# S5's outer products and the weights' sums on GpSimd, two generators for S5's constants, and a tail with GLU and projection A as separate stages

## The chip, the cores and the metric

The kernel runs on one core of one Trainium2 chip. The metric is the device time of one execution in microseconds (us); lower is better. One core has a matrix engine (TensorE, in the rows PE, its weight loads PEld), a vector engine (VectorE, DVE), a scalar engine (ScalarE, ACT), GpSimd (POOL) and a queue that only issues transfers (SyncE, SP). Each works through its own instructions in the order in which the program issued them; semaphores join them.

## The reference, cut to what matters

One layer of a hybrid encoder, for one prompt of 2048 frames and for eight streams of 16 frames, 1024 channels wide.

```python
h = rmsnorm(x, ln_g)
u_a, z_a, u_b, z_b, g_a, g_b = split(h @ w_in)        # 512 512 1024 1024 1024 1024 columns
y_a, s5_new = s5_mixer(u_a, s5_h0, ...)               # 32 groups of 16 channels, 64 complex states
y_a = gelu(y_a)
y_a = y_a * sigmoid(y_a @ w_glu + b_glu)              # GLU
p_a = (y_a * silu(z_a)) @ w_pa                        # projection A
xc, conv_new = causal_conv(u_b, conv_buf, conv_w, conv_b)
y_b, lru_new = rglru(xc, lru_h0, wa, ba, wx, bx, lam)
p_b = (y_b * silu(z_b)) @ w_pb                        # projection B
m = sigmoid(g_a) * p_a + sigmoid(g_b) * p_b
out = rmsnorm(x + m @ w_out, final_gain)
```

## The kernel before

Every product is made of three float16 matmuls, high by high, high by low and low by high (lines 161 to 163). The frames lie in five tiles, four of 512 columns (n = 0 to 3) and one of 128 for the streams (n = 4). The stages follow each other on PE:

1. **Norm and u_a** (lines 533 to 599). For each tile n and each of four column blocks m, `proj` makes a block of u_a. In the blocks m = 2 and 3 the next tile is transposed by `trans_tile`, two of its eight slabs k in the middle of the block's product (the argument `between`) and two behind it, all through the three PSUM buffers "a". Meanwhile `params` makes S5's parameters, on GpSimd for the most part.
2. **Direct gate blocks** (lines 1308 to 1355). Four columns of gate B, while `t_forms` builds sums of the frames for what follows. `lru_states` (line 648) brings the old states into place by transposes into one PSUM buffer; its copy into `dT` stands between the first transpose and the next.
3. **Branch B** (`run_pair`, lines 1361 to 1396). Sixteen pairs of column blocks, in turn one of branch B ("b") and one of gates ("g"). A pair has 15 slots: seven products of a Winograd scheme over the frames' first half, one slot for the streams, seven products for the second half; a product is 12 matmuls of 512 columns. The weights of the next pair are loaded at slot 5 (`load_pair`) and made into eight forms by `w_forms` (line 778) from slot 8 on: four sums of 128x512 by `tt` on DVE, each then split by ACT (`high`) and DVE (`low`).
4. **S5 beside projection B** (lines 1639 to 1685). For each tile and eight blocks m a product with w_pb; between them come the sixteen `s5_run` tasks, one for two groups each. The loop behind it, `while tasks or low or due`, goes on until every task is over, and so does `tail_start`, which waits for all `s5_run` tasks and then loads w_out and makes `glu_prep(0)`.
5. **Tail** (lines 1704 to 1833). `glu_prep(n)` splits S5's output into high and low; `ga_tile(n)` makes four GLU blocks and then eight blocks of projection A; `out_tile(n)` makes the output product, 24 matmuls for each half row block. The order of tiles is 0, 1, 4, 2, 3, and `BESIDE` says what runs beside which output tile.

Work beside the products is dealt out by a planner. `pump(budget)` (line 683) runs what is due, then lets the generators in `tasks`, and then those in `low`, issue their next piece until the budget of the slot is spent; a yielded number or `Step` costs that much of it, and `Later(k)` lets k turns pass at no cost. In `low` stand `w_spill` (line 1140, 44 blocks of later weights, loaded, split and stored to DRAM) and two generators `s5_prep` (line 1203), which make the constants of the sixteen `s5_run` tasks: parameters are loaded; `outer` (line 1234) makes "wb" and later "wc", each by four products of 128x256 and one sum of 128x512; "wb" is transposed on PE; "wc" is multiplied on PE (line 1282); the result is split, stored to `kpD` by GpSimd (line 1296), and read back by SP as `dd` (line 1301). An `s5_run` task starts when its constants are in the set `prepared`. The second generator waits until branch B is over. `place` is the slot in a b pair (1 to 15) or 15 more in a g pair (16 to 30); `NO_SPILL` and `NO_PREP` are places at which these generators rest.

Of the kernel before, what the change touches and what calls it, by code (L numbers as in the profile page):

```python
# [17 lines left out]
P = 128  # L18
# [29 lines left out]
def build(tc, I, O):  # L48
# [30 lines left out]
    with ExitStack() as es:  # L79
# [121 lines left out]

        def proj(W, n, tag="mm", between=None):
            p = ps(tag)[:, :TILES[n][1]]
            for k in range(KB):
                passes(p, W(k), hT(n, k), k == 0, k == KB - 1)
                if k == 3 and between:
                    between()
            return p
# [9 lines left out]
        with ExitStack() as p1x:  # L218
# [66 lines left out]
            def trans_tile(n, ks=range(KB)):  # L285
                t0, w = TILES[n]
                for k in ks:
                    pt = ps("ab"[k % 2])[:, :w]
                    for i in range(w // P):
                        transp(pt[:, P * i:P * i + P], xts[n, i][:, P * k:P * k + P])  # L290
                    evac_h(n, k, pt)
# [255 lines left out]
            for n in range(4):  # L547
# [8 lines left out]
                for m in range(4):  # L556
                    early = n < 3 and m >= 2
                    p = proj(lambda k: wua[m][:, k], n,
                             between=(lambda: trans_tile(n + 1, range(4 * m - 8, 4 * m - 6))) if early else None)
                    if 0 < n < 3 and m == 1:  # L560
# [16 lines left out]
                    if n < 3:  # L577
                        if m == 0:
                            st = stats()
                            for i in range(4):  # L580
                                norm_sums(n + 1, i, st)
                        if n == 0 and m == 1:
                            norm_root(1, st)
                        if m == 1:
                            for i in range(4):
                                norm_scale(n + 1, i, st)
                            if n == 0:
                                split_ua(3)
                        if m >= 2:
                            trans_tile(n + 1, range(4 * m - 6, 4 * m - 4))  # L590
                    if n == 0 and m == 3:
# [56 lines left out]
        def lru_states():  # L648
            pp = ps("b")
            transp(pp[0:64, 256:272], dn)  # L650
            V.tensor_copy(out=dT, in_=pp[0:64, 256:272])
            transp(pp[:, 0:64], rows2)
            for i in range(2):
                transp(pp[:, 64 + 96 * i:160 + 96 * i], rows3[i])
            ts(lrs[:, 0:64], pp[:, 0:64], LS)
            V.tensor_copy(out=lrs[:, 64:256], in_=pp[:, 64:256])
# [121 lines left out]
        def w_forms(raw, W):  # L778
# [17 lines left out]
            high("A11", A11)  # L796
            tt(t, A21, A22, ADD)
            yield 0.7
            low("A11", A11)
            high("S1", t)  # L800
            yield 0.7
            low("S1", t)
            tt(t, t, A11, SUB)
            high("A12", A12)
            yield 1.3
            low("A12", A12)
            high("S2", t)
            yield 0.7
            low("S2", t)
            tt(t, A12, t, SUB)  # L810
            yield 1.3
            high("A21", A21)
            high("S4", t)
            yield 0.2
            low("A21", A21)
            tt(A21, A11, A21, SUB)
            low("S4", t)
            yield 2.0
            high("S3", A21)
# [316 lines left out]

        NO_SPILL = range(15, 22)
        NO_PREP = range(13, 22)

# [55 lines left out]
        def scratch(nm):  # L1195

            if nm == "t":
                return temp[:, 0:512].rearrange("p (j g h t) -> p j g h t", j=2, g=2, h=16)
            if nm == "w":
                return temp[:, 512:1024].rearrange("p (a r c) -> p a r c", a=2, r=2)  # L1200
            return temp[:, 1024:1280].rearrange("p (r c) -> p r c", r=2)

        def s5_prep(second):
# [9 lines left out]
            dd = None  # L1213
            while second and branch_b:
                yield Later(1)
            while todo:
# [17 lines left out]
                def outer(nm, pr_, pi_, m1, m2):  # L1234
                    w_ = gt([P, 2, 2, 16, 8], name=nm)
                    t = gt([P, 2, 2, 16, 8], name="t") if branch_b else scratch("t")
                    for dst, po, mo in ((w_, pr_, m1), (t, pi_, m2)):
                        for j in range(2):
                            if nm == "wb":
                                pe = pw_(po, 8 - 8 * j, 16 - 8 * j)[:, :, ::-1]  # L1240
                            else:
                                pe = pw_(po, 8 * j + 1, 8 * j + 9)
                            tt(dst[:, j], pe[:, :, None, :].to_broadcast([P, 2, 16, 8]),
                               mat(mo)[:, :, :, None].to_broadcast([P, 2, 16, 8]), MUL)
                    tt(w_, w_, t, ADD)
                    return w_.rearrange("p j g h t -> p j g (h t)")
# [3 lines left out]
                wb = outer("wb", O_PR, O_PI, O_B, O_BS)  # L1250
                yield Step(2.2)
                yield Later(1)
                p = ps("a", (P, 4, P))
# [13 lines left out]
                wc = outer("wc", O_PR, O_PI, O_C, O_CS)  # L1267
                yield Step(2.8)
                yield Later(1)
                wcs = gt([P, 2, 2, 2, P], F16, name="wcs")  # L1270
# [341 lines left out]
        def glu_prep(n):  # L1612
# [4 lines left out]
            for m in range(4):  # L1617
# [9 lines left out]
                yield  # L1627

        def tail_start():

            while len(tasks) > 1 or done["spill"] < 44:
                yield Later(1)
            for i in range(4):
                wo.append(page_load(page_b("t1", (2, 2, D), "wo"), woD[i]))
                yield Later(1)
            for _ in glu_prep(0):
                yield Step(1.4)
# [48 lines left out]
        load_w(wpa, wpaD[1])  # L1686
        so2 = out_states2()

# [14 lines left out]

        def ga_tile(n):
            w = TILES[n][1]
            zq = [tload(zaD, m, n, "qz") for m in range(2)]
            yA[n] = page_a("h", (4, 2, w), "yA") if n < NT - 1 else gt([P, 4, 2, w], F16, "yA")
            for m in range(4):
# [12 lines left out]
                parts(yA[n][:, m], z, 1.0)  # L1721
                yield
            flush()
            gq = [(tload(gaD, m, n, "ga"), tload(mbD, m, n, "mb")) for m in range(2)]
# [74 lines left out]

        def chain(*gens):  # L1800
            for g in gens:
                yield from g

        flush()
        ahead = glu_prep(1)
        for i, _ in enumerate(ga_tile(0)):
# [5 lines left out]
            if i > 7:  # L1812
                next(ahead, None)


        BESIDE = {0: ([1], 2, [4, 2]), 1: ([4, 2], 3, [3]), 4: ([], 0, []), 2: ([3], 2, []), 3: ([], 0, [])}
        for n in TAIL:
            flush()
            gas, steps, preps = BESIDE[n]
            nxt = chain(*[ga_tile(x) for x in gas])  # L1820
            ahead = chain(*[glu_prep(x) for x in preps])
            for i, _ in enumerate(out_tile(n)):
                pump(0)
                for _ in range(steps):
                    next(nxt, None)
                    pump(0)
                if i > 3 or len(preps) > 1:
                    next(ahead, None)
            for _ in nxt:
                pump(0)  # L1830
            for _ in ahead:
                pump(0)
# [33 lines left out]
```

## Time and profile before

| | us |
|---|---|
| median of three timed runs | 1571.83 (1568.13 to 1572.23) |
| profiled execution, device time | 1577.57 |
| its span, first to last instruction | 1575.8 |
| PE busy in the span | 1462.2 (93%) |
| DVE busy | 1039.9 (66%) |
| ACT busy | 816.1 (52%) |
| POOL busy | 275.3 (17%) |

The busy time of PE counts an instruction from its start to its modelled end; matmuls overlap, so a long instruction of 0.38 us may be followed by the next after 0.22 us. [...] What a stage loses is its idle PE time and, of the busy time, the share by which the clock was below 1.00.

### The profile page before, as it was taken

How to read it: one execution, taken by the hardware profiler on the slowest of the kernel's cores; microseconds unless marked ns; L12 is line 12 of the kernel's file. 1: busy time of each engine (PE TensorE's matmuls, PEld its weight loads, DVE VectorE, ACT ScalarE, POOL GpSimd, SP SyncE). 2: the span in 40 equal slices, each digit the busy share in tenths (PEclk: the TensorE clock that was granted, in tenths of full speed). 3: DMA queues.
4: the chain of work that ended last, by engine and by line, in shares of the span. 5: the costliest groups of instructions: out<-in, count | busy, mean ns of one | idle time of the engine just before them, and what ended most of it. 6: DMA issues, size and time to landing. Idle time of an engine off the chain costs nothing.

```text
span 1575.8 us, 22665 instructions
## 1 busy us (share of the span) xinstructions
PE 1462.2 (93%) x8168; PEld 735.3 (47%) x8168; DVE 1039.9 (66%) x2137; ACT 816.1 (52%) x1524; POOL 275.3 (17%) x557
## 2 busy tenths in 40 slices
PE   5989999999999899999999999999983789989997
PEld 3544445444444454444444444555463334444443
DVE  5445785778786677869788784656544776657543
ACT  6542434766767385876867581433234443533322
POOL 0591010120202011110201112334333000000000
PEclk9889999999999999999999999999995889999999
DMA  8216212332422233331413369985856805333431
GB/s 204 85 59 235 81 62 79 98 126 65 139 66 106 86 104 121 102 123 61 156 61 103 110 227 320 331 282 161 308 175 227 310 1 187 99 123 120 174 108 54
DMA packets 168489, 222.20 MB, mean 141 GB/s; under 512 B 39258, under 2 KB 117738, under 8 KB 166328
## 3 DMA queue, kind: packets, MB, share of 16 engines
q1 hardware_dynamic: 144440, 150.96, 29.8%
q0 software_dynamic: 23936, 69.79, 11.9%
q8 instruction: 64, 1.05, 0.3%
q14 instruction: 49, 0.40, 0.1%
HBM read 133.85 MB, written 86.84 MB: 140 GB/s over the span
## 4 chain that ended last, share of the span: by engine, by line
PE 71%; DVE 9%; ACT 6%; DMA 6%; issue 5%; SPq 1%; POOL 1%; DVEq 0%; ACTq 0%; POOLq 0%
PE ps_mm L161 18%; PE ps_mm L162 18%; PE ps_mm L163 18%; PE ps_mm L1775 3%; PE ps_mm L1773 3%; PE ps_mm L1774 3%; DMA wraw<-w_in 1%; PE ps_a L172 1%; ACT L74 1%; DVE yh L53 1%; PE ps_a L1282 1%; DVE xc L65 1%; PE ps_a L162 1%; PE ps_a L161 1%; PE ps_a L163 1%
## 5 line engine op out<-in xcount | busy, mean ns | idle before, releaser
L161 PE MATMUL ps_mm<-T,wf 128*128 128x512 f16 x512 | 194.8, 380 | 11.6 <-ACT ub L74 8.1
L163 PE MATMUL ps_mm<-T,wf 128*128 128x512 f16 x512 | 194.6, 380 | 1.0 <-DVE wf L65 1.0
L162 PE MATMUL ps_mm<-T,wf 128*128 128x512 f16 x512 | 194.7, 380 | 0.0
L162 PEld LDWEIGHTS <-wf 128*128 128x128 f16 x1232 | 120.8, 98 | 124.7 <-issue 15.7
L161 PEld LDWEIGHTS <-wf 128*128 128x128 f16 x1232 | 120.7, 98 | 117.2 <-issue 5.0
L163 PEld LDWEIGHTS <-wf 128*128 128x128 f16 x1232 | 120.8, 98 | 116.6 <-DVE wf L65 2.6
L161 PE MATMUL ps_mm<-h,wf 128*128 128x512 f16 x448 | 170.6, 381 | 2.0 <-ACT wf L74 2.0
L163 PE MATMUL ps_mm<-h,wf 128*128 128x512 f16 x448 | 170.4, 380 | 0.7 <-DVE wf L65 0.7
L162 PE MATMUL ps_mm<-h,wf 128*128 128x512 f16 x448 | 170.5, 381 | 0.0
L1775 PE MATMUL ps_mm<-wo,M 128*128 128x512 f16 (+2 forms) x264 | 99.2, 377 | 5.3 <-DVE M L65 5.3
L1773 PE MATMUL ps_mm<-wo,M 128*128 128x512 f16 (+2 forms) x264 | 99.1, 377 | 0.0
L1774 PE MATMUL ps_mm<-wo,M 128*128 128x512 f16 (+2 forms) x264 | 99.0, 376 | 0.0
L161 PE MATMUL ps_mm<-Y,wpb 128*128 128x512 f16 x256 | 97.8, 382 | 0.0
L163 PE MATMUL ps_mm<-Y,wpb 128*128 128x512 f16 x256 | 97.7, 382 | 0.0
L162 PE MATMUL ps_mm<-Y,wpb 128*128 128x512 f16 x256 | 97.6, 381 | 0.0
L74 ACT ACT_TABLE_LOAD x62 | 79.5, 1283 | 6.1 <-PE ps_mm L163 4.3
L65 DVE SCALAR_TENSOR_TENSOR gb<-gb,ps_mm 128x512 f32<-128x512 f32 (+1 forms) x40 | 24.2, 605 | 86.5 <-PE ps_mm L163 63.9
L74 ACT ACTIVATE gs<-ps_mm 128x512 f32<-128x512 f32 (+1 forms) x92 | 48.5, 537 | 55.6 <-PE ps_mm L163 54.4
L65 DVE SCALAR_TENSOR_TENSOR xc<-ub,PC,xc 128x512 f32<-128x512 f32 x96 | 71.8, 749 | 2.6 <-ACT xc L74 0.3
L65 DVE SCALAR_TENSOR_TENSOR xo<-ps_mm,xo 128x512 f32<-128x512 f32 (+2 forms) x35 | 23.9, 681 | 73.8 <-PE ps_mm L1775 73.7
L65 DVE SCALAR_TENSOR_TENSOR wf<-wraw,wf 128x512 f16<-128x512 f32 (+1 forms) x82 | 55.7, 696 | 17.4 <-ACT wf L74 17.2
L162 PE MATMUL ps_mm<-yA,wt 128*128 128x512 f16 (+1 forms) x160 | 55.7, 356 | 11.0 <-DVE yA L65 7.1
(326 smaller groups left out, 3301.5 us busy)
## 6 DMA issues: line engine op xcount, KB each, us to landing
wraw<-w_in SPq DMA_DIRECT2D x38, 512.0 KB, 4.2
sp<-sD SPq DMA_DIRECT2D x16, 768.0 KB, 5.1
xt<-x_prompt SPq DMA_DIRECT2D x16, 512.0 KB, 4.2
gbD<-gs POOLq DMA_DIRECT2D x32, 256.0 KB, 2.3
ybD<-y POOLq DMA_DIRECT2D x32, 256.0 KB, 3.0
gaD<-gs POOLq DMA_DIRECT2D x32, 256.0 KB, 2.5
Y<-ybD SPq DMA_DIRECT2D x8, 1024.0 KB, 11.1
gb<-gbD SPq DMA_DIRECT2D x32, 256.0 KB, 6.9
```

Of the source, the lines that this page charges most:

```text
L53: V.tensor_tensor(out=out, in0=a, in1=b, op=op)
L65: V.scalar_tensor_tensor(out=out, in0=a, scalar=s, in1=b, op0=op0, op1=op1)
L74: S.activation(out=out, in_=a, func=f, **kw)
L161: PE.matmul(p, lhsT=a[:, 0], rhs=b[:, 0], start=first, stop=False, skip_group_check=more)
L162: PE.matmul(p, lhsT=a[:, 0], rhs=b[:, 1], start=False, stop=False, skip_group_check=more)
L163: PE.matmul(p, lhsT=a[:, 1], rhs=b[:, 0], start=False, stop=last, skip_group_check=more)
L172: PE.matmul(out, lhsT=in_, rhs=ident[0:k, 0:k], start=True, stop=True, is_transpose=True)
L1282: PE.matmul(o[:, 16 + P * j:16 + P * j + w], lhsT=lb, rhs=wc[:, j, g].rearrange("p (h t) -> p t h", t=8)[:, 0:w // 16], start=True, stop=True)
L1773: PE.matmul(p, lhsT=lh[0], rhs=w_[:, 0, c], start=(k == 0), stop=False)
L1774: PE.matmul(p, lhsT=lh[0], rhs=w_[:, 1, c], start=False, stop=False)
L1775: PE.matmul(p, lhsT=lh[1], rhs=w_[:, 0, c], start=False, stop=(k == KB - 1))
```

## The change

- `proj` loses `between`; `trans_tile` makes four slabs in a row behind the blocks m = 2 and 3, and takes its PSUM buffers from "a" and "mm" in turn.
- In `lru_states` the copy to `dT` moves behind all transposes.
- The four sums of `w_forms` go to GpSimd (`gtt` for `tt`), and their costs in the planner fall by 2.4 for a pair in all.
- All products and sums of `outer` go to GpSimd; the planner is charged 3.6 instead of 7.8 for a task's constants, and three turns pass before PE uses a product. Their scratch "t" is always a tile of its own.
- The second `s5_prep` starts as soon as one set of constants is prepared, in branch B.
- `NO_SPILL` grows from places 15 to 21 to 13 to 21, `NO_PREP` from 13 to 21 to 11 to 21.
- `tail_start` prepares tiles 0 and 1. `ga_tile` is cut into `glu_tile` and `pa_tile`; the tail starts with GLU of tiles 0 and 1, then projection A of tile 0 with the preparation of tiles 4 and 2 beside it, then two blocks of projection A of tile 1, then the output tiles. `out_states2` moves from ahead of the tail to behind its third GLU block.

```diff
-        def proj(W, n, tag="mm", between=None):
+        def proj(W, n, tag="mm"):
             p = ps(tag)[:, :TILES[n][1]]
-            for k in range(KB):
-                passes(p, W(k), hT(n, k), k == 0, k == KB - 1)
-                if k == 3 and between:
-                    between()
+            gemm(p, W, lambda k: hT(n, k), KB)
...
-                    pt = ps("ab"[k % 2])[:, :w]
+                    pt = ps(("a", "mm")[k % 2])[:, :w]
...
-                            trans_tile(n + 1, range(4 * m - 6, 4 * m - 4))
+                            trans_tile(n + 1, range(4 * m - 8, 4 * m - 4))
...
             transp(pp[0:64, 256:272], dn)
-            V.tensor_copy(out=dT, in_=pp[0:64, 256:272])
             transp(pp[:, 0:64], rows2)
             for i in range(2):
                 transp(pp[:, 64 + 96 * i:160 + 96 * i], rows3[i])
+            V.tensor_copy(out=dT, in_=pp[0:64, 256:272])
...
-            tt(t, A21, A22, ADD)
-            yield 0.7
+            gtt(t, A21, A22, ADD)
+            yield 0.1
...
-            tt(t, t, A11, SUB)
+            gtt(t, t, A11, SUB)
...
-            tt(t, A12, t, SUB)
+            gtt(t, A12, t, SUB)
...
-            tt(A21, A11, A21, SUB)
+            gtt(A21, A11, A21, SUB)
...
-        NO_SPILL = range(15, 22)
-        NO_PREP = range(13, 22)
+        NO_SPILL = range(13, 22)
+        NO_PREP = range(11, 22)
...
-            while second and branch_b:
+            while second and not prepared:
                 yield Later(1)
...
-                            tt(dst[:, j], pe[:, :, None, :].to_broadcast([P, 2, 16, 8]),
+                            gtt(dst[:, j], pe[:, :, None, :].to_broadcast([P, 2, 16, 8]),
                                mat(mo)[:, :, :, None].to_broadcast([P, 2, 16, 8]), MUL)
-                    tt(w_, w_, t, ADD)
+                    gtt(w_, w_, t, ADD)
...
                 wb = outer("wb", O_PR, O_PI, O_B, O_BS)
-                yield Step(2.2)
-                yield Later(1)
+                yield Later(3)
...
                 wc = outer("wc", O_PR, O_PI, O_C, O_CS)
-                yield Step(2.8)
-                yield Later(1)
+                yield Step(0.8)
+                yield Later(2)
...
-            for _ in glu_prep(0):
+            for _ in chain(glu_prep(0), glu_prep(1)):
                 yield Step(1.4)
...
+        pa = {n: pa_tile(n) for n in TAIL}
+        for i, _ in enumerate(chain(glu_tile(0), glu_tile(1))):
             pump(0)
             if i < 2:
                 xload(i)
+            if i == 2:
+                so2 = out_states2()
+        ahead = chain(glu_prep(4), glu_prep(2))
+        for i, _ in enumerate(pa[0]):
+            pump(0)
+            next(ahead, None)
             if i == 1:
                 out_states3(so2)
+        for _ in range(2):
+            next(pa[1])
+            pump(0)
...
-        BESIDE = {0: ([1], 2, [4, 2]), 1: ([4, 2], 3, [3]), 4: ([], 0, []), 2: ([3], 2, []), 3: ([], 0, [])}
+        BESIDE = {0: (pa[1], glu_tile(4), glu_tile(2)), 1: (pa[4], pa[2]), 4: (glu_tile(3),), 2: (pa[3],), 3: ()}
```

## Rows read from the trace of the kernel before

**Rows 1.** Windows: length, busy us (instructions) of each engine, granted clock, DMA share.
```profile
36.00:147.00 111.00, 98.06 (x526) 52.48 (x526) 52.84 (x127) 48.76 (x95) 62.73 (x176) 0.89 0.29 103
147.00:300.00 153.00, 147.14 (x780) 70.64 (x781) 111.24 (x192) 68.88 (x124) 14.60 (x27) 0.97 0.29 93
300.00:958.00 658.00, 644.30 (x3609) 317.20 (x3608) 507.68 (x935) 459.34 (x803) 104.92 (x194) 1.00 0.34 114
958.00:1166.00 208.00, 203.80 (x1365) 112.58 (x1363) 113.42 (x326) 66.46 (x174) 72.27 (x122) 0.99 0.78 267
1166.00:1225.00 59.00, 24.66 (x229) 21.36 (x230) 24.55 (x86) 21.54 (x54) 18.77 (x32) 0.65 0.66 220
1225.00:1290.00 65.00, 54.62 (x219) 22.36 (x218) 49.58 (x76) 28.34 (x38) 1.05 (x2) 0.84 0.48 173
1290.00:1420.00 130.00, 121.44 (x642) 58.41 (x641) 79.95 (x180) 53.14 (x100) 0.00 (x0) 0.95 0.37 129
```

**Rows 2.** Who PE waited for, 1166 to 1225: total us, times, longest.
```profile
PE ps_a L1486 <- ACT hst L74: 18.8, 3, 10.0
PE ps_mm L161 <- ACT yh L74: 8.9, 1, 8.9
```

**Rows 3.** Line 1282, eight matmuls a task's constants: 250 to 960, then 960 to 1225.
```profile
L1282 PE MATMUL ps_a<-wc,par x80: 382/386/413, 270.6 to 947.6; 128*32 128x128 f32 x40, 128*32 128x112 f32 x40
...
L1282 PE MATMUL ps_a<-wc,par x48: 382/386/413, 1054.3 to 1169.5; 128*32 128x128 f32 x24, 128*32 128x112 f32 x24
```

**Rows 4.** Who PE waited for, 36 to 147.
```profile
PE ps_a L172 <- DVE xt L69: 13.2, 4, 8.3
```

**Rows 5.** Who PE waited for, 147 to 300.
```profile
PE ps_a L172 <- DVE dTe L651: 3.8, 1, 3.8
```

**Rows 6.** Who PE (first row) and ACT (other rows) waited for, 300 to 958.
```profile
PE ps_mm L161 <- ACT ub L74: 8.1, 5, 4.7
...
ACT wf L74 <- DVE wt L53: 19.0, 13, 6.2
...
ACT wq L74 <- DMA wr<-w_pb: 8.2, 1, 8.2
```

**Rows 7.** DVE groups by shape: count, busy us, mean ns, idle before.
```profile
L53 DVE TENSOR_TENSOR wt<-wt,wraw 128x512 f32<-128x512 f32 x16 | 11.1, 692 | 0.6
...
L53 DVE TENSOR_TENSOR wc<-par 128x256 f32<-128x256 f32 x32 | 12.0, 415 | 0.0
```

**Rows 8.** POOL groups by shape, the same columns.
```profile
L56 POOL TENSOR_TENSOR e<-pw 128x256 f32<-128x256 f32 x4 | 2.6, 657 | 0.2
...
L56 POOL TENSOR_TENSOR bst<-e 128x512 f32<-128x512 f32 x1 | 1.3, 1267 | 0.1
```

**Rows 9.** SP's own waits over the span, then SP's issues in order of time.
```profile
SPq L1301 <- DMA kpD<-kf: 214.7, 16, 34.1
...
522.97 2.73 SPq L1301 DMA_DIRECT2D dd<-kpD  x4
525.80 1.16 SPq L144 DMA_DIRECT2D wraw<-w_in  x2
```

**Rows 10.** DVE, then POOL, in order of time: start, us.
```profile
91.51 0.68 DVE L65 SCALAR_TENSOR_TENSOR sp_t<-sp_t 128x8 f32<-128x8 f32 x1
...
91.45 0.72 POOL L56 TENSOR_TENSOR pw<-e 128x256 f32<-128x256 f32 x1
```

**Rows 11.** DVE groups by shape, 1225 to 1290.
```profile
L53 DVE TENSOR_TENSOR yh<-ya,yh 128x256 f16<-128x256 f32 x15 | 17.1, 1314 | 0.0
L65 DVE SCALAR_TENSOR_TENSOR gl<-gl,ya 128x256 f32<-128x256 f32 x12 | 6.7, 602 | 7.2 <-ACT gl L74 7.0
```

**Rows 12.** Who PE waited for, 1225 to 1420.
```profile
PE ps_mm L1775 <- DVE M L65: 5.3, 3, 2.1
```

**Rows 13.** PE in order of time: start and modelled length of two matmuls.
```profile
1151.34 0.38 PE L161 MATMUL ps_mm<-Y,wpb 128*128 128x512 f16 x1
1151.56 0.38 PE L162 MATMUL ps_mm<-Y,wpb 128*128 128x512 f16 x1
```

More of the change, by code (lines that the diff above doesn't have):

```diff
@@ L556, in build @@
                 for m in range(4):
-                    early = n < 3 and m >= 2
-                    p = proj(lambda k: wua[m][:, k], n,
-                             between=(lambda: trans_tile(n + 1, range(4 * m - 8, 4 * m - 6))) if early else None)
+                    p = proj(lambda k: wua[m][:, k], n)
                     if 0 < n < 3 and m == 1:
@@ L802, in w_forms @@
             low("S1", t)
-            tt(t, t, A11, SUB)
+            gtt(t, t, A11, SUB)
             high("A12", A12)
-            yield 1.3
+            yield 0.7
             low("A12", A12)
@@ L809, in w_forms @@
             low("S2", t)
-            tt(t, A12, t, SUB)
-            yield 1.3
+            gtt(t, A12, t, SUB)
+            yield 0.7
             high("A21", A21)
@@ L815, in w_forms @@
             low("A21", A21)
-            tt(A21, A11, A21, SUB)
+            gtt(A21, A11, A21, SUB)
             low("S4", t)
-            yield 2.0
+            yield 1.4
             high("S3", A21)
@@ L1195, in scratch @@
         def scratch(nm):
-            if nm == "t":
-                return temp[:, 0:512].rearrange("p (j g h t) -> p j g h t", j=2, g=2, h=16)
             if nm == "w":
@@ L1235, in outer @@
                     w_ = gt([P, 2, 2, 16, 8], name=nm)
-                    t = gt([P, 2, 2, 16, 8], name="t") if branch_b else scratch("t")
+                    t = gt([P, 2, 2, 16, 8], name="t")
                     for dst, po, mo in ((w_, pr_, m1), (t, pi_, m2)):
@@ L1627, in glu_prep, with chain @@
                 yield
+        def chain(*gens):
+            for g in gens:
+                yield from g
         def tail_start():
@@ L1686, in build @@
         load_w(wpa, wpaD[1])
-        so2 = out_states2()
         def parts(d, t, f):
@@ L1702, in flush, with glu_tile @@
                 pump(0)
-        def ga_tile(n):
+        def glu_tile(n):
             w = TILES[n][1]
@@ L1722, in ga_tile, with pa_tile @@
                 yield
+        def pa_tile(n):
+            w = TILES[n][1]
             flush()
@@ L1798, in rest @@
             defer(1, squares)
[L1800 to L1806, printed above, removed]
+        pa = {n: pa_tile(n) for n in TAIL}
+        for i, _ in enumerate(chain(glu_tile(0), glu_tile(1))):
             pump(0)
@@ L1809, in build @@
                 xload(i)
+            if i == 2:
[4 more added lines that the diff above has]
+            next(ahead, None)
             if i == 1:
                 out_states3(so2)
-            if i > 7:
-                next(ahead, None)
-        BESIDE = {0: ([1], 2, [4, 2]), 1: ([4, 2], 3, [3]), 4: ([], 0, []), 2: ([3], 2, []), 3: ([], 0, [])}
+        for _ in range(2):
+            next(pa[1])
+            pump(0)
+        BESIDE = {0: (pa[1], glu_tile(4), glu_tile(2)), 1: (pa[4], pa[2]), 4: (glu_tile(3),), 2: (pa[3],), 3: ()}
         for n in TAIL:
             flush()
-            gas, steps, preps = BESIDE[n]
-            nxt = chain(*[ga_tile(x) for x in gas])
-            ahead = chain(*[glu_prep(x) for x in preps])
+            nxt = chain(*BESIDE[n])
+            ahead = glu_prep(3) if n == 1 else iter(())
             for i, _ in enumerate(out_tile(n)):
                 pump(0)
-                for _ in range(steps):
+                if n == 2 and not i:
+                    continue
+                for _ in range(2):
                     next(nxt, None)
                     pump(0)
-                if i > 3 or len(preps) > 1:
-                    next(ahead, None)
+                next(ahead, None)
             for _ in nxt:
-                pump(0)
-            for _ in ahead:
                 pump(0)
```

## The prediction

> **What bounds the kernel.** [...] For 1166 to 1225 that is 34.3 + 24.66 x 0.35 = 42.9 us. The same sum gives 12.9 + 10.8 = 23.7 for 36 to 147; 5.9 + 4.4 = 10.3 for 147 to 300; 13.7 for the 658 us of branch B; 6.2 for 958 to 1166; 10.4 + 8.7 = 19.1 for 1225 to 1290; and 8.6 + 6.1 = 14.7 for 1290 to 1420. The change takes no matmul away; it can only move these losses. So next I read whom PE waited for in each stage: in the 42.9 us, S5's `hst`, 18.8 us in three waits, then `yh`, 8.9 us [rows 2]; in stage one the scaled frames, 13.2 us [rows 4]; then the copy to `dT`, 3.8 us [rows 5]. Last I read what that S5 work had waited for: ten tasks' constants go through line 1282 in branch B (80 of 128 matmuls), six later, up to 1169 [rows 3], when projection B is almost over. The last `s5_run` tasks run alone behind it.
>
> **S5 and projection B, 958 to 1225.** I stepped the planner's rules turn by turn through the program, with the yields, places and costs of the code; no times enter. For the code before, ten sets of constants are begun in branch B, as in [rows 3], and the last S5 task is over 21 turns after projection B. For the changed code, with 3.6 instead of 7.8 charged for a set, 2.4 less for each `w_forms`, and two generators, the sixteenth set is prepared three turns behind branch B's end; the S5 tasks end 11 turns before projection B does, and `glu_prep(0)` and the greater part of `glu_prep(1)` are issued inside it. So both waits of [rows 2] go. I leave 3 us for the change to the tail and keep the 6.2 us that the stage loses at its start: 49.1 becomes 9, **-40** (-46 to -25; the worse end if S5's last tasks overrun by some 15 us). The six sets' own PE work moves to branch B and costs there what it saves here.
>
> **Stage one.** Without `between`, PE does the second half of a block, 12 matmuls of 0.216 us [rows 13] = 2.6 us, before it asks for the scaled frames; of 13.2 us in four waits this takes up to 2.6 each, and the half-clock stretches behind the short ones with it. Transposing four slabs in a row leaves less time for the last slabs' evictions, which may cost 1 us for a tile. **-9** (-16 to -2).
>
> **lru_states.** PE's next transpose waits for a copy out of the same buffer. With the copy last, the 3.8 us go [rows 5], and the half clock behind them; DVE has idle time there. **-6** (-7 to -3).
>
> **Sums and outer products.** DVE loses 64 sums of 0.692 us = 44 us, and in branch B ten tasks' two products each (4 x 0.415 + 0.692 = 2.35 us) = 47 us [rows 7]. POOL gets 64 x 1.267 = 81 us, and 32 outer products of 4 x 0.657 + 1.267 = 3.9 us = 125 us [rows 8]: 206 us, so that it is busy 311 instead of 105 of 658 us [rows 1]. It isn't full, but it works in order. Three things lie on PE's path:
> - *Two outer products in a row.* By the stepped planner two fall into one or two neighbouring slots in five g pairs, where both generators come out of their rest at once at place 22. That is 7.8 us by [rows 8]. The weight sum behind them is read by ACT one slot later (some 2.8 us), so ACT stands, and with it the evictions PE needs; `wb` and `wc` are read by PE itself three turns later (8.4 us).
> - [...] A DVE operation of 8 columns issued just behind a POOL product took 0.68 us and ended with it [rows 10]: the two exclude each other where both read SBUF. If each POOL operation also waits for part of a DVE one (0.25 us, a third of 0.692), an outer product takes 5.2 us and a pair 10.4. Then ACT stands some 7 us in two pairs and 2 to 4 us in three more, of which PE sees most in the former and half in the latter; with direct waits of 2 to 3 us and half clock: **+26**.
> - *SP's read-back.* `dd` stands on SP until `kpD` has landed, 214.7 us in 16 waits [rows 9], and all loads queue behind it. Once, when it was issued just ahead of `load_pair`, SP went on only at 523; ACT waited 8.2 us for a transfer, and PE had its longest wait in branch B, 4.7 us [rows 6], some 8.6 us lost with what followed. The stepped planner puts `dd` right ahead of `load_pair` in four pairs (two before the change), with the same neighbours as that one in two: 2 x 8.6 + 6 less the 11 there now = **+12**.
>
> Against these stands that ACT waits 19.0 us for the sums now, behind a busy DVE [rows 6], of which I give **-5**. Together **+33** (-5, if POOL's work fits into waits that exist anyway, to +70).
>
> [...]
>
> **The tail.** Beside PE, DVE has to split S5's output, 8 x 1.314 = 10.5 us a tile, and spends about 2 x 0.602 + 2 x 0.69 = 2.6 us on a GLU block and 3 x 0.69 = 2.1 on a block of projection A [rows 7, 11], each of 12 matmuls = 2.6 us of PE. Now it has 10.5 + 4 x 2.6 + 8 x 2.1 = 38 us ahead of the first output block, against 31 of PE: the stage loses 19.1, with 5.3 us waiting for M [rows 12]. Changed, eight GLU blocks, ten of projection A and two full and one quarter preparations come first: 21 + 21 + 24 = 66 us of DVE against 18 x 2.6 = 47 of PE. So the start still is DVE's, and I expect 25 us lost there. What follows has slack: GLU is always a few blocks ahead of its projection A, so the 14.7 us of 1290 to 1420 become about 3. 33.8 becomes 28: **-6** (-20 to +10).
>
> **Sum.** -40 - 9 - 6 + 33 - 6 = -28 on the profiled execution's 1577.57 us, or 1550; that execution lay 5.7 us above the median of the runs, so the forecast is 1571.8 - 28 = **1544**.
>
> **Rivals.**
> - *POOL hides.* The pairs' delays fall into slots where ACT and DVE are ahead, and loads arrive in time: branch B at +3 instead of +33. For it: ACT and DVE are busy 70 and 77% in branch B, and PE loses only 13.7 us of 658. Against it: the wait of [rows 9]. 1514.
> - *Branch B becomes bound by POOL and DVE excluding each other (slower).* DVE's 508 - 91 + 12 us for six more tasks' splits, plus POOL's 206, are 635 of 658 us if nothing overlaps. It decides once each of 64 sums, held behind outer products and DVE, keeps PE 1 us beyond its slot: 64 + 12 = +76 instead of +33, so 1587. For it: every sum is read one slot later. Against: a sum alone takes 1.27 us, and most pairs hold one outer product ahead of a sum, not two.
> - *S5 still overruns.* The stage's transfers (DMA share 0.78, [rows 1]) or the S5 tasks' own waits keep the last ones until behind projection B, and half the 42.9 us stay: 1544 + 20 = 1564. Against: the first ten tasks kept pace with projection B.
>
> **Chances.** Forecast (1525 to 1560) 0.50; POOL hides 0.17; S5 overruns 0.15; branch B bound 0.13 (of which 0.04 end level); the rest is spread. About 0.3% is what a measurement of this kernel can tell from no change: faster than 1567 0.80, within 0.07, slower than 1576.5 0.13. The range of 1508 to 1577 holds the first three cases and the lower end of the fourth.
>
> **What would show it.** Right: line 1282's 128 matmuls all by about 970; no `hst` wait over 5 us after 1100, and projection B followed by GLU within 5 us; no `dT` wait; PE waits in branch B on ACT `ub` and `gs` and on POOL `wb` or `wc` that sum to 20 to 40 us; DVE's yA and M waits within 60 us of the first GLU block. Wrong: PE idle under 20 us in branch B, or over 60; S5 still behind projection B; a tail whose first stage loses much less than 25 us.

## The result, and the profile after

| | us |
|---|---|
| median after | 1552.05 (1549.32 to 1554.67) |
| median before, measured beside it | 1572.03 (1568.13 to 1574.71) |
| after / before | 0.9875, interval 0.9843 to 0.9906 |
| profiled execution after, and its span | 1549.53, 1547.7 |

The change makes the kernel 20 us faster (15 to 25 by the interval), where 28 was forecast. The two profiled executions differ by 28.0 us, which is the forecast's sum; the medians differ by less, since the profile before lay 5.7 us above the median of the runs shown first and the profile after lies 2.5 below its own. The total is near the forecast, but two of its five terms are far off, in opposite directions. That shows when the windows of the stages are set beside [rows 1]. The boundaries are moved to the same places in the program: `u_a` up to 126, direct gate blocks up to 220, branch B up to 1003 (ten us into projection B, as 958 was before), S5 and projection B up to GLU at 1218, the first output block at 1275. Only the last boundary, 1410, is not at the place of 1420 in the kernel before: some 75 more PE instructions lie ahead of it.

```profile
0.00:36.00 36.00, 26.77 (x180) 17.06 (x181) 21.83 (x59) 26.20 (x51) 1.01 (x6) 1.00 0.87 223
36.00:126.00 90.00, 82.22 (x451) 43.52 (x448) 50.74 (x119) 45.70 (x93) 62.85 (x176) 1.00 0.29 102
126.00:220.00 94.00, 92.98 (x495) 44.73 (x496) 69.49 (x112) 35.84 (x63) 15.35 (x23) 0.98 0.38 129
220.00:1003.00 783.00, 718.93 (x3972) 350.80 (x3970) 580.17 (x877) 517.86 (x905) 353.92 (x458) 0.97 0.35 114
1003.00:1218.00 215.00, 211.07 (x1515) 121.65 (x1514) 100.79 (x324) 59.57 (x185) 71.11 (x117) 1.00 0.78 270
1218.00:1275.00 57.00, 52.09 (x221) 22.12 (x220) 55.90 (x91) 40.47 (x53) 1.05 (x2) 0.90 0.76 257
1275.00:1410.00 135.00, 131.57 (x717) 63.74 (x715) 88.74 (x186) 52.80 (x98) 0.00 (x0) 1.00 0.36 121
```

The columns are those of [rows 1]. Two stretches of the kernel before, its first 36 us and its direct gate blocks, are needed as well:

```profile
0.00:36.00 36.00, 20.57 (x101) 12.24 (x101) 19.52 (x52) 24.37 (x49) 1.01 (x6) 0.97 0.91 221
147.00:248.00 101.00, 96.09 (x496) 45.67 (x497) 70.22 (x115) 36.52 (x63) 10.87 (x20) 0.95 0.30 98
```

By the sum of the prediction (length less PE busy, plus PE busy times the clock that is missing) each stage loses:

| stage | before | after | difference | forecast |
|---|---|---|---|---|
| start and stage one | 16.0 + 23.7 | 9.2 + 7.8 | -22.7 | -9 |
| direct gate blocks (`lru_states`) | 9.7 | 2.9 | -6.8 | -6 |
| branch B | 14.6 | 85.6 | +71.0 | +33 |
| S5 and projection B | 49.1 | 3.9 | -45.2 | -40 |
| tail up to 1420, after to 1410 | 33.8 | 13.5 | -20.3 | -6 |

What lies behind the tail's last boundary loses 9.7 us before and 8.3 after. With that the differences sum to -25.4, against -28.1 of the span; the clock is printed to a hundredth, and half of one is 3.9 us in the window of 783. At a granted clock of 1.00 the matmuls of [rows 13] begin 0.22 us apart; behind the wait of [rows 5], from 230 to 234 us of the kernel before, the clock is 0.50 and they begin 0.43 us apart. Branch B costs twice what was forecast, and stage one and the tail give back nearly as much more.

Whom PE waited for in branch B of the kernel after (220 to 1000; total us, times, longest):

```profile
PE ps_mm L161 <- ACT gs L74: 23.0, 11, 5.8
PE ps_mm L161 <- DMA Y<-ybD: 11.0, 2, 9.3
PE ps_mm L161 <- ACT ub L74: 10.3, 7, 3.5
PE ps_a L162 <- DVE xs L53: 7.3, 4, 4.3
PE ps_a L1274 <- POOL wc L56: 5.0, 4, 2.0
PE ps_a L172 <- POOL wb L56: 2.8, 2, 2.2
```

And ACT in the same stage, whose waits in [rows 6] were 19.0 us for the sums:

```profile
ACT wf L74 <- POOL wt L56: 48.7, 27, 4.9
...
ACT wq L74 <- DMA wr<-w_out: 10.5, 2, 5.5
```

PE waits little for POOL itself (7.8 us). It waits longer for ACT's evictions `gs` and `ub`, and ACT had waited for the weight sums on POOL.

### The profile page after: what moved, and what is told of

Read it like the earlier page. It is cut to its first block, busy times and chain, and to the rows that moved or that the text cites. A ratio compares the mean times of both kernels' runs of the same rounds, so it can differ in the third digit from the quotient of the medians.

```text
span 1547.7 us, 22800 instructions
## 1 busy us (share of the span) xinstructions
PE 1446.3 (93%) x8168; PEld 724.0 (47%) x8168; DVE 1034.2 (67%) x1913; ACT 815.5 (53%) x1526; POOL 505.3 (33%) x781
## 4 chain that ended last, share of the span: by engine, by line
PE 48%; issue 15%; DVE 11%; POOL 10%; ACT 7%; DMA 7%; SPq 2%; POOLq 0%; DVEq 0%; ACTq 0%
PE ps_mm L161 11%; PE ps_mm L163 11%; PE ps_mm L162 11%; PE ps_mm L1773 4%; PE ps_mm L1771 4%; PE ps_mm L1772 4%; DVE xc L65 2%; POOL wt L56 2%; POOL t L56 2%; POOL wc L56 1%; POOL wb L56 1%; DVE wf L65 1%; ACT L74 1%; POOL wraw L56 1%; ACT d L74 1%
## 5 line engine op out<-in xcount | busy, mean ns | idle before, releaser
L161 PE MATMUL ps_mm<-T,wf 128*128 128x512 f16 x512 | 198.8, 388 | 34.8 <-ACT gs L74 23.0
L163 PE MATMUL ps_mm<-T,wf 128*128 128x512 f16 x512 | 198.7, 388 | 1.3 <-DVE wf L65 1.3
L162 PE MATMUL ps_mm<-T,wf 128*128 128x512 f16 x512 | 198.6, 388 | 0.0
L1773 PE MATMUL ps_mm<-wo,M 128*128 128x512 f16 (+2 forms) x264 | 98.0, 373 | 3.4 <-DVE M L65 3.4
L1771 PE MATMUL ps_mm<-wo,M 128*128 128x512 f16 (+2 forms) x264 | 98.0, 373 | 0.0
L1772 PE MATMUL ps_mm<-wo,M 128*128 128x512 f16 (+2 forms) x264 | 98.0, 373 | 0.0
L65 DVE SCALAR_TENSOR_TENSOR xc<-ub,PC,xc 128x512 f32<-128x512 f32 x96 | 79.9, 832 | 3.2 <-ACT xc L74 1.0
L65 DVE SCALAR_TENSOR_TENSOR wf<-wraw,wf 128x512 f16<-128x512 f32 (+1 forms) x82 | 64.8, 806 | 6.2 <-ACT wf L74 6.1
L1065 POOL DMA_DIRECT2D gbD<-gs x40 | 21.8, 546 | 134.4 <-ACT gs L74 134.3
L74 ACT ACTIVATE yo<-ps_a 128x256 f32<-128x256 f32 x64 | 14.7, 281 | 86.1 <-PE ps_a L1479 86.0
```

The costliest lines, as they stand in the source:

```text
L65: V.scalar_tensor_tensor(out=out, in0=a, scalar=s, in1=b, op0=op0, op1=op1)
L74: S.activation(out=out, in_=a, func=f, **kw)
L161: PE.matmul(p, lhsT=a[:, 0], rhs=b[:, 0], start=first, stop=False, skip_group_check=more)
L162: PE.matmul(p, lhsT=a[:, 0], rhs=b[:, 1], start=False, stop=False, skip_group_check=more)
L163: PE.matmul(p, lhsT=a[:, 1], rhs=b[:, 0], start=False, stop=last, skip_group_check=more)
L1065: G.dma_start(out=dst[m, :, t0:t0 + w], in_=t)
```

## The experiments

Five theories on branch B are named in the expectations. (A *theory* here is a guess at the cause, with the time that it would give.) **Q**: ACT and PE wait for results that stand in POOL's queue. **Pairs**: this happens where two outer products stand in neighbouring slots. **X**: POOL and DVE exclude each other, so that DVE is stretched. **H**: POOL's queue is merely held, whatever the work does, so that sums and stores behind it come late. **G**: two generators bunch S5's work, and SP's read-back `dd` with it, whichever engine makes the products. A and B, on the read-back, are told where they first stand. The kernel before, measured beside each group of runs, had medians from 1568.1 to 1572.0, so that differences of some 4 us between runs of two groups say nothing.

| kernel | median us | ratio to before (interval) |
|---|---|---|
| after | 1552.05 | 0.9875 (0.9843 to 0.9906) |
| both_dve: sums and products on DVE | 1521.07 | 0.9681 (0.9655 to 0.9706) |
| sums_dve: only the sums on DVE | 1550.8 | 0.9868 (0.9842 to 0.9893) |
| outer_dve: only the products on DVE | 1488.63 | 0.9477 (0.9451 to 0.9502) |
| dummy_pool: both_dve, all of it a second time on POOL | 1604.34 | 1.0213 (1.0187 to 1.0238) |
| dummy_outer: outer_dve, products a second time on POOL | 1559.19 | 0.9923 (0.9897 to 0.995) |
| dummy_memset: outer_dve, memsets on POOL | 1527.98 | 0.9728 (0.9696 to 0.976) |
| one_gen: after, second generator later | 1535.26 | 0.9782 (0.9756 to 0.9808) |
| dd_later: after, read-back four turns later | 1518.33 | 0.9669 (0.9645 to 0.9693) |
| outer_dve_dd: both | 1498.55 | 0.9554 (0.9537 to 0.9571) |
| both_dve_dd | 1519.34 | 0.9687 (0.9667 to 0.9707) |
| stage1: before, stage one and `lru_states` alone | 1552.66 | 0.9897 (0.9877 to 0.9917) |
| tail_only: before, the tail alone | 1551.16 | 0.989 (0.9859 to 0.9922) |

### Which of the two moves to GpSimd costs

**both_dve** puts back both moves, with the planner's old charges, and keeps the rest of the change:

```diff
-            gtt(t, A21, A22, ADD)
-            yield 0.1
+            tt(t, A21, A22, ADD)
+            yield 0.7
...
-                            gtt(dst[:, j], pe[:, :, None, :].to_broadcast([P, 2, 16, 8]),
+                            tt(dst[:, j], pe[:, :, None, :].to_broadcast([P, 2, 16, 8]),
...
-                    gtt(w_, w_, t, ADD)
+                    tt(w_, w_, t, ADD)
```

> The changed kernel (1552) with the four weight sums and all outer products back on DVE, and their old costs in the planner; two generators, the new rests, stage one and the tail stay. Theory Q (ACT and PE wait for results that stand in POOL's queue): branch B loses some 25 us less, 1527 (1517 to 1537). [...] Theory G (two generators bunch S5's work and SP's read-back, whatever the engine): within 8 us of 1552, or above it, as DVE has 119 us more to do.

**sums_dve** is the first part of this diff alone, **outer_dve** the second alone, each with the old charges of what it puts back, outer_dve also with the old turns between a product and its use by PE.

> The changed kernel with only the four weight sums of a pair back on DVE. Theory Q: ACT's 49 us of waiting for `wt` from POOL go back to some 19 us behind DVE, and most PE waits on ACT `gs` with them: 1537 (1530 to 1545). Theory X: 64 POOL operations fewer of 224, so a third of its share: 1544 to 1550. Theory G: 1548 to 1558.

> The changed kernel with only the outer products back on DVE (old costs and turns). Theory Q: no sum stands behind an outer product any more, so ACT waits for `wt` less than 20 us, and PE no longer for `wb` and `wc`: 1535 (1528 to 1543). Theory X: 160 POOL operations fewer, so two thirds of its share: 1535 to 1545, not to be told from Q by the time but by DVE's mean durations. Theory G: 1548 to 1560.

Measured: 1521.07, 1550.8 and 1488.63; no theory had put outer_dve under 1528. G falls as a cause by itself: both_dve and outer_dve keep the two generators and are 31 and 63 us under the kernel after. The products on POOL cost 1552.05 - 1488.63 = 63 us. The sums on POOL gain 1521.07 - 1488.63 = 32 us, but only while the products are on DVE; beside them they gain nothing (1550.8 against 1552.05). In each of these runs the engine and the planner's charges change together. Seen the other way, the products on POOL cost 30 us (1550.8 - 1521.07) where the sums are on DVE, and 63 where the sums stand behind them on POOL. Branch B of outer_dve, from 221 to 927, then DVE's products in it and four other groups of DVE (count, busy us, mean ns, idle before):

```profile
221.00:927.00 706.00, 694.38 (x3929) 343.63 (x3928) 583.40 (x1020) 508.61 (x890) 217.24 (x285) 1.00 0.36 117
```

```profile
L53 DVE TENSOR_TENSOR t<-par 128x256 f32<-128x256 f32 x62 | 23.2, 413 | 3.1 <-DMA sD<-wcs 3.1
L53 DVE TENSOR_TENSOR wb<-wb,t 128x512 f32<-128x512 f32 x16 | 12.4, 775 | 0.6
L53 DVE TENSOR_TENSOR wb<-par 128x256 f32<-128x256 f32 x32 | 11.9, 411 | 0.0
L53 DVE TENSOR_TENSOR wc<-wc,t 128x512 f32<-128x512 f32 x15 | 11.3, 755 | 0.5
L53 DVE TENSOR_TENSOR wc<-par 128x256 f32<-128x256 f32 x30 | 11.2, 415 | 0.0
...
L65 DVE SCALAR_TENSOR_TENSOR xc<-ub,PC,xc 128x512 f32<-128x512 f32 x96 | 72.0, 750 | 3.7 <-ACT xc L74 1.4
L65 DVE SCALAR_TENSOR_TENSOR wq<-wr,wq 128x512 f16<-128x512 f32 x34 | 25.6, 752 | 0.6 <-ACT wq L74 0.6
L65 DVE SCALAR_TENSOR_TENSOR q<-a,q 128x512 f32<-128x512 f32 x32 | 21.8, 680 | 1.8 <-ACT a L74 1.8
L69 DVE TENSOR_SCALAR lrs<-gx 128x8 f32<-128x8 f32 x8 | 1.4, 175 | 0.3
```

The stage loses 11.6 us, though DVE is busy for 583.4 of 706. DVE's products are 23.2 + 12.4 + 11.9 + 11.3 + 11.2 = 70 us of it. In the kernel after they are gone from DVE, and yet DVE is busy for 580.2 us there, as the window above shows. The other groups have taken the 70 us up. Three of these four in the kernel after:

```profile
L65 DVE SCALAR_TENSOR_TENSOR xc<-ub,PC,xc 128x512 f32<-128x512 f32 x96 | 79.9, 832 | 3.2 <-ACT xc L74 1.0
L65 DVE SCALAR_TENSOR_TENSOR wq<-wr,wq 128x512 f16<-128x512 f32 x38 | 35.9, 945 | 3.7 <-ACT wq L74 3.7
L69 DVE TENSOR_SCALAR lrs<-gx 128x8 f32<-128x8 f32 x8 | 12.4, 1550 | 0.3
```

An operation of eight columns takes 1550 instead of 175 ns in the mean. How, the order of time shows, in the kernel after; first DVE, then POOL (start, us):

```profile
293.64 3.33 DVE L65 SCALAR_TENSOR_TENSOR q<-a,q 128x512 f32<-128x512 f32 x1
...
293.99 1.24 POOL L56 TENSOR_TENSOR wb<-par 128x256 f32<-128x256 f32 x2
295.19 1.23 POOL L56 TENSOR_TENSOR t<-par 128x256 f32<-128x256 f32 x2
```

A DVE operation that takes 0.68 us in the mean in outer_dve ends 0.55 us behind the last of four products on POOL, of which the first began 0.35 us after it: it stood for all four. The prediction had let DVE stand for one POOL operation at a time.

### Does the work on POOL cost, or the wait for its results?

**dummy_pool** and **dummy_outer** leave results and their readers as they are in both_dve and outer_dve, and let POOL make the same a second time into a tile that nobody reads; **dummy_memset** lets POOL fill that tile instead, for about as long. What the second and third add to outer_dve:

```diff
+                    z_ = gt([P, 2, 2, 16, 8], name="dz")
...
+                            gtt(z_[:, j], pe[:, :, None, :].to_broadcast([P, 2, 16, 8]),
+                                mat(mo)[:, :, :, None].to_broadcast([P, 2, 16, 8]), MUL)
+                    gtt(z_, z_, z_, ADD)
```

```diff
+                    z_ = gt([P, 2, 2, 16, 8], name="dz")
...
+                            for _ in range(2):
+                                G.memset(z_, 0.0)
```

> As both_dve, and POOL makes the same weight sums and outer products a second time, into tiles that nobody reads. So POOL is as busy as in the changed kernel, and its stores stand behind this work, but no result of it is waited for. Theory Q: within 6 us of both_dve. Theory X: 15 to 30 us above both_dve, with DVE's mean durations of `xc` and `wf` as in the changed kernel (832 and 806 ns instead of 749 and 696).

> As outer_dve (1489), and POOL makes the outer products a second time, into tiles that nobody reads; the planner's costs are those of outer_dve. Theory Q (it was PE and ACT waiting for the products themselves): within 8 us of 1489. Theory X (what matters is that POOL reads and writes SBUF beside DVE): 1525 to 1555, with DVE's means raised. Theory H (POOL's queue is held, so the weight sums and stores behind the products come late): 1525 to 1555 too, but with DVE's means near those of outer_dve and ACT waiting for `wt`.

> As outer_dve, and in the place of each outer product POOL also does eight memsets of 128x512 into a tile that nobody reads, about as long as an outer product (8 x 0.52 = 4.2 us), but with no reads. Theory H (the queue is held): as dummy_outer, 1525 to 1555. [...] Theory Q: near 1489.

Measured: dummy_pool 1604.34, 83 us over both_dve, where X had 15 to 30. dummy_outer 1559.19, 71 us over outer_dve, for products that nobody waits for, and with outer_dve's charges and turns: Q falls as a cause of the products' own cost, and the charges do not make it. dummy_memset 1527.98, 39 us over outer_dve, at the lower end of H's range. Branch B of dummy_outer, with DVE's first group of products, and of dummy_memset, with POOL's memsets and the group `xc`:

```profile
219.00:993.00 774.00, 711.47 (x3927) 347.00 (x3926) 661.90 (x1013) 509.01 (x887) 341.69 (x439) 0.98 0.32 106
...
L53 DVE TENSOR_TENSOR t<-par 128x256 f32<-128x256 f32 x62 | 60.7, 1018 | 8.1 <-DMA kpD<-kf 5.5 <-DMA sD<-wcs 2.6
```

```profile
222.00:958.00 736.00, 701.37 (x3926) 344.49 (x3924) 576.48 (x1016) 508.08 (x889) 343.01 (x532) 0.99 0.34 111
...
L1240 POOL MEMSET dz<- 128x512 f32 x248 | 130.7, 527 | 16.3 <-DMA sD<-wcs 3.8
L65 DVE SCALAR_TENSOR_TENSOR xc<-ub,PC,xc 128x512 f32<-128x512 f32 x96 | 77.7, 810 | 3.7 <-ACT xc L74 1.4
```

With products, DVE's busy time rises from 583.4 to 661.9 us for the same work: X. With memsets of the same length on POOL (343.0 us busy, with products 341.7) it doesn't rise (576.5), though one group, `xc`, goes from 750 to 810 ns; what rises is ACT's wait for the sums, as H has it (dummy_memset):

```profile
ACT wf L74 <- POOL wt L56: 50.1, 29, 6.5
```

That wait was 32.8 us in outer_dve, and is 64.0 in dummy_outer. So of 71 us some 39 come with a held queue, and the other 32 with products, which stretch DVE. The split is rough: DVE makes its products just where POOL repeats them, so that these two meet more often than they would elsewhere (in dummy_outer the mean of `t` goes from 413 to 1018 ns, that of `xc` from 750 to 792), and `xc` in dummy_memset, 810 ns, shows that memsets aren't quite free for DVE. It agrees with the two costs above: 30 us where no weight sum can be held behind the products, 63 where they can.

### Two generators, and SP's read-back

**one_gen** holds the second generator until branch B is over, as before. **dd_later** puts four turns between the store to `kpD` and the read-back:

```diff
-            while second and not prepared:
+            while second and branch_b:
```

```diff
                     G.dma_start(out=kpD[q, g, :, :, 128:384], in_=kh[48 * g:48 * g + 16])
+                yield Later(4)
                 dd = q, gt([P, 2, 2, 256], F16, name="dd")
```

> The changed kernel (1552) with the second generator of constants held until branch B is over, as before; the products stay on POOL. No two outer products stand in neighbouring slots, but as with ten sets before, constants are still being made beside projection B. Theory of pairs, as predicted: branch B loses 26 us less, and S5 overruns projection B by some 20 to 40 us, so 1545 to 1565. Theory H or X: branch B's loss falls with the number of products in it (some ten of sixteen sets), 85 to about 60, and the overrun adds 20 to 40: 1550 to 1570. Branch B's loss is what tells them apart: near 55 or lower with no ACT wait for `wt` over 3 us in g pairs (pairs), or one third less with such waits left (H, X).

> The changed kernel (1552) with SP's read-back `dd` issued four turns later, so that `kpD` has landed or nearly so when SP comes to it. If SP's read-back costs what the prediction gave it (12 us, and the 11 us that projection B waits for Y behind it): 1530 (1522 to 1540). If the loads behind it are early enough anyway: 1545 to 1555.

Measured: one_gen 1535.26, 17 us under the kernel after and under all its ranges. Branch B loses 36 instead of 83 us by its windows, under the 55 that were named as the sign of the pairs. But ACT still waits for the sums, 36.2 us in all and 4.2 at the longest, and the run has some ten sets of products in branch B, no pairs and fewer read-backs all at once, so it can't tell the pairs from H and X. S5 overruns again, and PE waits in projection B for S5's input (942 to 1201), and as long again (9.2 us) for `hst`:

```profile
PE ps_a L1427 <- DMA u<-uD: 9.5, 1, 9.5
```

dd_later 1518.33, 34 us under the kernel after and below the 1522 to 1540 that were named. What it takes away is seen in the kernel after, first at branch B's end (SP's issues, then PE):

```profile
983.86 2.46 SPq L1293 DMA_DIRECT2D dd<-kpD  x4
986.37 1.14 SPq L1545 DMA_DIRECT2D Y<-ybD  x2
...
993.31 0.59 PE L161 MATMUL ps_mm<-Y,wpb 128*128 128x512 f16 x1 [9.33 <-DMA Y<-ybD]
993.69 0.63 PE L162 MATMUL ps_mm<-Y,wpb 128*128 128x512 f16 x1
994.12 0.63 PE L163 MATMUL ps_mm<-Y,wpb 128*128 128x512 f16 x1
```

SP could issue the load of Y only behind `dd`, for which it had waited 6.8 us, and PE stood for 9.33 us and then ran at half clock, matmuls 0.43 us apart instead of 0.22. In dd_later PE waits 3.9 us for Y. The same on the way, where SP had waited 20.9 us for `kpD`:

```profile
805.33 3.19 SPq L1293 DMA_DIRECT2D dd<-kpD  x4
...
810.07 1.14 SPq L1157 DMA_DIRECT2D wr<-w_out  x1
...
815.93 0.63 ACT L74 ACTIVATE wq<-wr 128x512 f16<-128x512 f32 x1 [5.53 <-DMA wr<-w_out]
```

ACT's waits for such loads fall from 19.8 us in the kernel after (10.5 of them above) to under 1 us. But the four turns also pull the generators apart. In the kernel after two outer products stand in a row on POOL, ACT waits for the sum behind them, and PE for ACT:

```profile
372.06 1.24 POOL L56 TENSOR_TENSOR wb<-par 128x256 f32<-128x256 f32 x2
...
376.21 1.74 POOL L56 TENSOR_TENSOR wc<-par 128x256 f32<-128x256 f32 x2
...
380.12 1.59 POOL L56 TENSOR_TENSOR wc<-wc,t 128x512 f32<-128x512 f32 x1
...
382.79 1.27 POOL L56 TENSOR_TENSOR wt<-wraw 128x512 f32<-128x512 f32 x1
...
384.10 0.63 ACT L74 ACTIVATE wf<-wt 128x512 f16<-128x512 f32 x1 [4.87 <-POOL wt L56]
...
391.70 0.58 PE L161 MATMUL ps_mm<-T,wf 128*128 128x512 f16 x1 [5.83 <-ACT gs L74]
```

This happens again from 861.6 on (PE's wait: 5.1 us). In dd_later such products stand 11 us apart at this place, and PE's waits for `gs` in branch B fall from 23.0 us:

```profile
PE ps_mm L161 <- ACT gs L74: 10.8, 10, 2.2
```

ACT's waits for the sums hardly fall (47.2 us, where they were 48.7), and PE's for `wc` rise from 5.0 to 9.4. So the 34 us come with less waiting for loads and for `gs`; that the latter is the pairs' parting is argued, as no run parts them by itself.

**outer_dve_dd** and **both_dve_dd** add the same line where the products are on DVE.

> The changed kernel with the outer products back on VectorE (1488.6 us by itself) and, in addition, four turns between S5's store to kpD and the issue of dd's read-back on SP (by itself 34 us in the changed kernel). Theory A, SP's read-back costs wherever it stands ahead of loads: the part of branch B's 18.8 us that such loads hold is saved too, 1472 to 1484 us. Theory B, the read-back costs only while the constants come late because GpSimd makes and stores them late: with the products on VectorE nothing is left to save, 1485 to 1493 us, and SP's wait for kpD falls without any effect on TensorE. Slower than 1493 us would mean that the four turns push S5's last constants past branch B.

> The changed kernel with both the sums and the outer products back on VectorE (1521.1 us) and four turns ahead of dd's read-back. GpSimd has little work here, so that its stores to kpD are early. Theory A (the read-back costs wherever it stands ahead of loads): 1500 to 1513 us. Theory B (it costs only while GpSimd is late): 1516 to 1526 us. Slower than 1526 us if VectorE, which is the busiest engine beside TensorE in this kernel, loses by four more turns ahead of S5's last tasks, of whose overrun 32.7 us stand behind projection B already.

Measured: 1498.55, which is 10 us slower than outer_dve, and 1519.34, where both_dve had 1521.07. A falls: its ranges ended at 1484 and 1513. SP waits for `kpD` as long in outer_dve as in the kernel after (202.8 us), and little waits for SP's loads, PE 3.3 us for Y and ACT 4.3:

```profile
SPq L1294 <- DMA kpD<-kf: 218.2, 15, 21.3
```

In both_dve PE waits 0.4 us for Y. The sum of SP's waits therefore tells nothing; what counts is whether a load behind it is late. B's range holds both_dve_dd, while outer_dve_dd came out over its 1493; B's mechanism, stores that POOL issues late, wasn't looked at by itself. The 10 us go with the four turns: S5's last constants, the matmuls that [rows 3] shows, end at 953.6 instead of 942.6, and with S5 eleven us late PE waits at the start of GLU in outer_dve_dd, where it had not waited in outer_dve:

```profile
PE ps_mm L161 <- ACT yh L74: 11.1, 1, 11.1
```

In both_dve S5's constants run to 1031, and this wait is:

```profile
PE ps_mm L161 <- ACT yh L74: 31.6, 1, 31.6
```

That is the greater part of the difference between both_dve and outer_dve: the sums on POOL gain mainly in that S5 is done in time. Whether the lower charge does that or the engine was not parted, as both move together.

### Stage one and the tail alone

**stage1** is the kernel before with the edits of `proj`, `trans_tile` and `lru_states`; **tail_only** is the kernel before with the new tail and `tail_start`. Both edits are those of the diff above.

> The kernel before with the change of stage one alone (no product cut in two, four slabs transposed in a row through two buffers) and the move of the copy to dT. By the profiles of before and after the two stages lose 20 and 7 us less: 1543 to 1549 us if the terms add up. If the products run earlier only to wait at the first loads of branch B, the gain is given back there: 1555 to 1566 us. By the prediction's sizes (9 and 6) 1557 us.

> The kernel before with the new tail alone (GLU and projection A as stages of their own, tail_start with the preparation of tiles 0 and 1, out_states2 behind the third GLU block); S5 still ends behind projection B. By the profiles the tail loses 21 us less: 1548 to 1555 us. If the second preparation in tail_start, which stands alone behind the last S5 task here, costs VectorE's 10.5 us ahead of the first GLU block: 1558 to 1564 us. By the prediction's size (6) 1566 us.

Measured: stage1 1552.66, 15.4 us under the 1568.1 of the kernel before beside it; tail_only 1551.16, 17 us under it. So stage1 lies between the 1557 by the prediction's sizes and the 1543 to 1549 by the profiles, and tail_only where the profiles put it. PE's wait for the scaled frames, 13.2 us in four [rows 4], is 2.1 us in four in stage1.

tail_only has stage one as before, with the same wait (13.3 us), and loses 31.6 us up to its first direct block, where the profiled kernel before lost 39.7: in the window from 36 its clock was 0.96 instead of 0.89. So, as far as two single executions can tell, 8 of the 22.7 us in the table lie in the one execution that was profiled, and the edit with `lru_states` is worth 15 by the times. The start of the tail in tail_only, 57 us (1216 to 1273) with DVE busy for 56.25, has the same shape as in the kernel after.

## Why the prediction was right, and where it was not

**S5 and projection B** (-40; -45.2): right, and for the reason given. The last of the 128 matmuls of the constants begins at 972.9, at branch B's end:

```profile
L1274 PE MATMUL ps_a<-wc,par x128: 382/386/422, 245.7 to 972.9; 128*32 128x128 f32 x64, 128*32 128x112 f32 x64
```

No wait for `hst` is left, and GLU begins 4 us behind projection B, as forecast.

**lru_states** (-6; -6.8): right; the wait of [rows 5] is gone.

**Stage one** (-9; -22.7 by the profiles): the mechanism was right, as [rows 4] said. By the times, stage1's 15.4 us are just the forecast's 9 + 6; the profiled execution before had lost more there than that of tail_only. So that execution's 5.7 us over the median, which the prediction had noted, seem to lie in this stage.

**The tail** (-6; -20.3, or -17 by tail_only): mis-sized. The prediction let DVE make 66 us of work ahead of the first output block. Between 1214 and 1275 it is busy for 57.4 us: 22.9 for the splits, where 24 were counted, and 34.5 for everything else, where 42 were counted for the blocks of GLU and projection A, some of whose operations run only behind that output block. PE begins on GLU while the splits still run, and the window from 1218 is 57 us long; PE loses 10.1 us in it, not 25. That the start is DVE's was right. PE's longest wait in the tail is for the first split, and the waits for M fell from 5.3 [rows 12] to 3.4 us:

```profile
PE ps_mm L161 <- ACT yh L74: 4.4, 2, 3.9
```

**Branch B** (+33; +71): the step that failed, in two of its terms.
- *DVE beside POOL.* The prediction let each POOL operation wait for a third of a DVE one, and priced that for the pairs alone; for DVE it counted 91 us of relief, of which it gave -5. There is no relief. DVE stands for up to four products at once (3.33 us), and with 70 us less of its own work it is as busy as in outer_dve. So products cost outside of pairs too, as the four from 293.99 on show, which stand in none; and dummy_outer's, which nobody waits for, cost 71 us. The pairs themselves, two of 9.7 and 9.9 us of POOL, took about what was forecast (10.4).
- *SP's read-back.* +12 was priced, and the Y load behind it at the stage's end was not seen: 9.3 us of waiting (3.9 in dd_later) and the half clock behind it (matmuls 0.43 us apart). The 8.6 us that it priced for a late `load_pair` stand in no row; PE was idle for 6.5 us from 520 to 560. Taken together with the parting of the pairs it is 34 us.
- The waits asked for as a sign, on `ub`, `gs`, `wb` and `wc`, sum to 10.3 + 23.0 + 2.8 + 5.0 = 41 us, at the forecast's end of 40; PE is idle for 64 us in the stage, over the 60 that were named as a sign of being wrong.

Thus the rival in which POOL and DVE exclude each other had the better price for this stage (+76) and its mechanism; its 1587 is missed only because the other stages gained more than anyone had counted. That the forecast's total is near is luck: the excess of branch B, 38 us, and what stage one and the tail gained beyond the forecast, 14 + 14 us by the profiles, and 5 in S5's stage, nearly cancel.

The prediction let POOL and DVE exclude each other where both read SBUF, from one DVE operation of 0.68 us [rows 10]. The runs agree with that as far as they go. The memsets, which read nothing, leave DVE's sum at 576.5 against 583.4 us, but for `xc`. DVE's groups with an input in PSUM keep their means beside the products (`gs` 686 ns in outer_dve, 684 in the kernel after and in dummy_outer; `ub` 687, 688 and 686), while that of `t` goes from 413 to 1018 ns in dummy_outer. To begin first did not spare DVE: the operation at 293.64 began 0.35 us ahead of the first product and yet stood for four POOL instructions in a row, 3.33 us.

**What stays open.** How the 34 us of dd_later are shared between the read-back and the parted pairs, what of the sums' 32 us is the engine's and what the planner's charge, and why the order of DVE and POOL alternates at some places (DVE 1.1 and POOL 0.9 to 1.1 us an operation at 376 to 380) and not at others.

## What to carry to other kernels

Work that was moved from DVE to POOL was not off DVE here: with 70 us of it gone, DVE was busy for 580.2 us in branch B, where it had been 583.4. Count how many operations POOL will issue without a pause beside DVE's, and price DVE, at the worst, as standing for all of them, as it did for the four from 293.99 on (3.33 us). Here sums of one operation each, spread out and with their lower charge, were worth moving once rows of five were not on POOL: moving the products back gives 1488.63 us, 5.2% under the kernel before and 4.1% under the kernel after, the best version found. Check the terms of a sum stage by stage even where the total is right, and before a queue's wait is called a cost, look for somebody who waits behind it.

## What was not expected of the hardware

- Four POOL products of 128x256 (0.63 to 0.65 us each) hold one DVE operation of 512 columns, the one at 293.64, for 3.33 us instead of 0.68, and one of eight columns for 1.55 us in the mean instead of 0.175.
- Removing 70 us of products from DVE left its busy time in branch B at 580.2 against 583.4 us.
- 131 us of POOL memsets leave DVE's busy time as it is (576.5 against 583.4 us), but cost the kernel 39 us, with ACT's wait for the sums on POOL up from 32.8 to 50.1 us.
- Four turns ahead of the read-back gained nothing in a kernel where SP waits 218.2 us for `kpD`, and 34 us in one where it waits 202.8.
